# State-space stage of a hybrid decoder step: B and C convolved before x, fixed convolution tiles, column copies on ScalarE, sums of squares emitted later

## The chip, the cores and the metric

One core of one Trainium2 chip runs one inference step of one decoder layer. The metric is the device time of one execution in microseconds (us), the median of three runs. PE is TensorE, ACT is ScalarE, DVE is VectorE, POOL is GpSimd, SP is the queue that issues most DMAs.

## The reference, cut to what matters

Each of 544 token rows (512 of a prompt, 8 sequences of 4 of a sample) goes through a feed-forward block, a mixing block of a state-space branch and an attention branch, a cross-attention over a memory, and a second feed-forward block, each with norms before and after. The change lies in the state-space branch and in the norms of the mixing and memory blocks:

```python
def causal_dwconv(xbc, buf, w, b):
    l = xbc.shape[1]
    xp = jnp.concatenate([buf.astype(xbc.dtype), xbc], axis=1)
    y = b
    for j in range(SSD_CONV_W):            # 4 taps
        y = y + w[j] * xp[:, j:j + l]
    return jax.nn.silu(y), xp[:, l:]
```

The convolution runs over 4096 channels: 2048 of x, 1024 of B and 1024 of C. Behind it, 32 heads in 8 groups are scanned in chunks of 128 tokens: `cb = C B^T` in a chunk, times a decay, times x; plus the state that is carried from chunk to chunk, which B and x make and C reads. The result is gated with silu(z) and normalised over the 256 channels of a group.

## The kernel before, in words

Activations stand with channels on the 128 partitions and the 544 tokens along the row. Matrix products are made from split operands (a rounded high part and the remainder, three products for each), so one product of 128 output channels over 1024 inputs is 48 matmuls of 256 or 288 columns (`mm`, L310). Weights come by `weights` (L251): two DMAs on SP into `wr`, a cast on ACT to `wh` (L270), a subtraction on DVE or POOL to `wl` (L271).

The program is written as generators that `weave` (L104) interleaves by a clock of estimated costs: `yield cost, delay` says how much PE work was emitted and how long its generator is to be left alone. The framework then makes from it one fixed list of instructions for each engine, in which it may move ready work ahead. Each engine works through its list in order.

The state-space stage is `ssd` (L1241). For each of the 8 groups (0 to 7 here) `fronts` runs `ssd_x` (L1291) and `ssd_z` (L1278), `tails` runs `ssd_y` (L1334), and beside them run the lists and the attention of the sample (`sample_select`, `sample_att`), whose rows are fetched by DMAs that POOL issues (L1613).

- `ssd_x` makes four products for a group, in the order x, x, B, C. The result in PSUM is copied by ACT into a tile `CB` of 604 columns (L1312); POOL writes three zeros ahead of the prompt (L1311), the old columns of the sample (L1315) and the new columns of the sample (L1316), and keeps the last columns for an output (L1317, L1318). The convolution is one ACT instruction (L1322) and three on DVE (L1324); then a tanh on ACT (L1326) and a last product on DVE (L1327) make `XO`. POOL copies the sample's columns of `XO` into `XS`, three times over for x and B (L1329).
- `ssd_y` starts with `pcb` (L1347, products of C and B by chunk) and `pbt` (L1353, B turned), then `pxt` (L1362, the two tiles of x turned) and `pcs` (L1379 and L1380, the sample's columns turned, and B times C of the sample). It ends with the norm of a group: `st` (L341, sums of squares), a chain of small DVE instructions in `rsqrt`, `zt` (L352) and `psr` (L355).

`bound` (L372) is the step between two blocks for one half of the tokens: it takes the norm behind the block (`sth` on `sqf`, L419, then `pgr`, L439), adds it to `hT`, sums the squares of the new `hT` on ACT and POOL (L369, L370, tile `sqh`), and takes the next norm (`sth` on `sqh`). `project` (L1762) calls it with a tile `rt` for w_out and for w_mo, once for each half.

Of the kernel before, what the change touches and what calls it, by code (L numbers as in the profile page):

```python
# [7 lines left out]
F32 = mybir.dt.float32  # L8
# [18 lines left out]
C_Z, C_X, C_B, C_C, C_DT, C_Q, C_K, C_V, C_QI, C_KI, C_WI, C_GS, C_GA = (  # L27
    0, 2048, 4096, 5120, 6144, 6176, 7200, 7456, 7712, 8224, 8288, 8296, 9320)
# [140 lines left out]
class Net:  # L169
# [202 lines left out]
    def bound(self, half, sq, post_g, pre_g, rt=None):  # L372


        nc, hT, y = self.nc, self.hT, self.y
        r0, n = HALF[half]
        sl = slice(r0, r0 + n)
        if post_g is not None:
            yield 0.0, 3.0
            r = yield from self.rms_h(sq, half)  # L380
        if pre_g is not None:
            acc = self.nw.tile([P, 288], F32, tag="sqh", name="sqh", bufs=2)
        for k in range(8):
            if post_g is not None:
                nc.vector.scalar_tensor_tensor(y[:, k, sl], y[:, k, sl], post_g[:, k:k + 1], r, op0=ALU.mult, op1=ALU.mult)
                (nc.gpsimd if k % 2 else nc.vector).tensor_tensor(hT[:, k, sl], hT[:, k, sl], y[:, k, sl], op=ALU.add)
            if pre_g is not None:
                self.sq_acc(acc, hT[:, k, sl], n, k == 0, last=(k == 7))
            if rt is not None:
                g = pre_g[:, k:k + 1]  # L390
                nc.scalar.activation(self.uh[:, k, sl], hT[:, k, sl], AF.Copy, scale=g)
                nc.vector.scalar_tensor_tensor(self.ul[:, k, sl], hT[:, k, sl], g, self.uh[:, k, sl].bitcast(F32), op0=ALU.mult, op1=ALU.subtract)
            yield 0.0, 1.0
        if pre_g is None:
            return
        yield 0.0, 4.0
        r = yield from self.rms_h(acc, half)
        if rt is not None:
            nc.scalar.copy(rt[:, sl], r)
            return  # L400
        for k in range(8):
            u = self.nw.tile([P, 288], F32, tag="u", name="u", bufs=2)
            nc.vector.scalar_tensor_tensor(u[:, :n], hT[:, k, sl], pre_g[:, k:k + 1], r, op0=ALU.mult, op1=ALU.mult)
            self.split(self.uh[:, k, sl], self.ul[:, k, sl], u[:, :n], nc.gpsimd if k % 4 == 3 else None)
            yield 0.0, 0.9
# [835 lines left out]
    def ssd(self, sel_ex, rounds):  # L1241
        nc, I = self.nc, self.I
        ex, fx = ExitStack(), ExitStack()
        self.sp = self.pool("ssd", ex)
        self.fp = self.pool("ssdf", fx)
        self.fr, self.zt = {}, {}
        self.r32 = self.sp.tile([P, 32], F32, name="r32")
        for q in range(4):
            nc.vector.tensor_copy(self.r32[q * 32:(q + 1) * 32], self.ident[q * 32:(q + 1) * 32, q * 32:(q + 1) * 32])
        fs = Flag()  # L1250
        f_x, f_y, f_z = ([Flag() for _ in range(8)] for _ in range(3))

        def tails():
            for g in range(8):
                yield from f_x[g].wait()
                yield from f_y[g].after(self.ssd_y(g, f_z[g]))

        def fronts():
            for g in range(8):
                if g >= 2:  # L1260
                    yield from f_y[g - 2].wait()
                yield from f_x[g].after(self.ssd_x(g))
                yield from f_z[g].after(self.ssd_z(g))
                if g in (1, 2):
# [26 lines left out]
    def ssd_x(self, g):  # L1291

        nc, I, sp = self.nc, self.I, self.sp
        fp = self.fp
        w_in = I["w_in"][0]
        wx = self.win(C_X + g * 256)
        h0 = []
        for i in range(2):
            h = sp.tile([P, 8, P], F32, tag="h0", name="h0", bufs=2)
            nc.sync.dma_start(h, I["state_ssm"][0][:, 4 * g + 2 * i:4 * g + 2 * i + 2].rearrange("b h p n -> (h p) b n"))  # L1300
            h0.append(h)
        XO = []
        xt = sp.tile([P, 320], F32, tag="XS", name="XS", bufs=2)
        XS = [xt[:, q * 96:q * 96 + (96 if q < 3 else 32)] for q in range(4)]
        for q in range(4):
            ct = (2 * g, 2 * g + 1, 16 + g, 24 + g)[q]
            if q == 2:
                wb = self.weights(("bc", g), [w_in[:, C_B + g * P:C_B + (g + 1) * P], w_in[:, C_C + g * P:C_C + (g + 1) * P]], 8)
            ps = yield from self.mm(wx if q < 2 else wb, self.xs, (q % 2) * P)
            CB = fp.tile([P, 604], F32, tag="CB", name="CB", bufs=2)  # L1310
            nc.gpsimd.memset(CB[:, 0:3], 0.0)  # L1311
            nc.scalar.copy(CB[:, 3:547], ps)  # L1312
            sb = CB[:, 547:603].rearrange("p (b j) -> p b j", b=8)
            raw = CB[:, 515:547].rearrange("p (b j) -> p b j", b=8)
            nc.gpsimd.tensor_copy(sb[:, :, 0:3], self.sc[:, ct, :].rearrange("p (b j) -> p b j", b=8))  # L1315
            nc.gpsimd.tensor_copy(sb[:, :, 3:7], raw)  # L1316
            nc.gpsimd.tensor_copy(self.ncv[:, ct, 0:3], CB[:, 512:515])  # L1317
            nc.gpsimd.tensor_copy(self.ncv[:, ct, 3:27].rearrange("p (b j) -> p b j", b=8), raw[:, :, 1:4])  # L1318
            pool = sp if g % 2 else fp
            xo = pool.tile([P, 600], F32, tag=f"XO{q}", name=f"XO{q}")  # L1320
            cw = lambda j: self.convw[:, j * 32 + ct:j * 32 + ct + 1]
            nc.scalar.activation(xo, CB[:, 0:600], AF.Identity, scale=cw(0), bias=self.convb[:, ct:ct + 1])  # L1322
            for j in range(1, 4):
# [2 lines left out]
            nc.scalar.activation(th, xo, AF.Tanh)  # L1326
            nc.vector.scalar_tensor_tensor(xo, th, 1.0, xo, op0=ALU.add, op1=ALU.mult)  # L1327
            r = 3 if q < 3 else 1
            nc.gpsimd.tensor_copy(XS[q].rearrange("p (r b t) -> p r b t", r=r, b=8),  # L1329
                                  xo[:, 544:600].rearrange("p (b j) -> p b j", b=8)[:, :, 3:7].unsqueeze(1).broadcast_to([P, r, 8, 4]))  # L1330
            XO.append(xo)
        self.fr[g] = (XO, XS, h0)

    def ssd_y(self, g, z):  # L1334
        nc, I, O, sp = self.nc, self.I, self.O, self.sp
        XO, XS, h0 = self.fr[g]
# [8 lines left out]
        ps = self.ps1("pcb")  # L1345
# [5 lines left out]
        ps = self.ps1("pbt")  # L1351
        for c in range(4):
            nc.tensor.transpose(ps[:, c * P:(c + 1) * P], BO[:, c * P:(c + 1) * P], self.ident)  # L1353
        Bt = sp.tile([P, 4, P], F32, tag="hT_", name="Bt", bufs=2)
        nc.scalar.copy(Bt.rearrange("p a b -> p (a b)"), ps)
        hcol = lambda t: t.rearrange("p (c h) -> p c h", c=4)[:, :, 4 * g:4 * g + 4]
        xd = sp.tile([P, 4, 4, 64], F32, tag="xd", name="xd")
        xe = sp.tile([P, 4, 4, 64], F32, tag="xe", name="xe")
        for i in range(2):
            ps = self.ps1("pxt")  # L1360
# [36 lines left out]
        Bb = sp.tile([96, 8, P], F32R, tag="Bb", name="Bb")  # L1397
        for b in range(8):
            nc.scalar.activation(Bb[:, b, :], Bs.bitcast(F32), AF.Copy, scale=self.bmask[:, b:b + 1])
        yield 0.5, 5.0  # L1400
        CZ = sp.tile([P, 288], F32, tag="CZ", name="CZ")
        nc.gpsimd.memset(CZ, 0.0)
        nc.gpsimd.tensor_copy(CZ.rearrange("p (b x) -> p b x", x=36)[:, :, :4], XS[3].rearrange("p (b t) -> p b t", b=8))
# [676 lines left out]
```

## Time and profile before

| | |
|---|---|
| median of 3 runs | 2214.59 us (2214.11 to 2221.61) |
| the profiled execution | 2221.14 us, span 2219.4 us |
| PE busy | 2112.4 us, 95% of the span |
| DVE, ACT, POOL busy | 1319.2, 947.8, 457.9 us |
| state-space stage | about 830 to 1400 us of the span |
| mean granted TensorE clock | 0.974 |

PE is busy nearly all the time, so a change is worth what it takes from or adds to PE's idle time, and from the time in which PE runs at the lower of its two clocks. The granted clock is given as a share of 2.4 GHz: 0.50 is 1.2 GHz.

### The profile page before, as it was taken

To read this page: it belongs to the slowest core of one execution; us is meant where nothing else is said; L and a number is where in the kernel's file an instruction comes from. 1 tells how busy PE (TensorE), PEld (TensorE's weight loads), DVE (VectorE), ACT (ScalarE), POOL (GpSimd) and SP (SyncE) were. 2 spreads that over 40 slices of the span, in tenths; PEclk is the share of its full clock that TensorE was granted. 3 is DMA by queue.
4 is the path that set the end of the run, shared out by engine and by line. 5 is a ranking of instruction groups with operands and counts; after the bars stand their busy time and mean duration, and the time that the engine had idled before them with its cause. 6 is when DMAs were issued, how large, how long until landed. Compare 5 with 4: busy or idle time off the path is not lost.

```text
span 2219.4 us, 41174 instructions
## 1 busy us (share of the span) xinstructions
PE 2112.4 (95%) x16675; PEld 1967.7 (89%) x16675; DVE 1319.2 (59%) x2711; ACT 947.8 (43%) x1757; POOL 457.9 (21%) x555
## 2 busy tenths in 40 slices
PE   7999999999999999999999999999999979999998
PEld 7999999998887779888778788999987879999998
DVE  6543334574788889886675678554663475423445
ACT  6323345345336665444345355332535343222233
POOL 0000011132123202235564451012320320000011
PEclk9999999999999999999899899999999989999999
DMA  6424565447432233345455545564444433233243
GB/s 194 128 82 127 172 209 187 120 124 223 141 118 78 83 93 100 116 146 177 125 158 163 152 143 166 174 201 148 139 161 142 150 116 115 71 92 95 82 123 106
DMA packets 320106, 301.70 MB, mean 136 GB/s; under 512 B 25416, under 2 KB 290632, under 8 KB 318868
## 3 DMA queue, kind: packets, MB, share of 16 engines
q1 hardware_dynamic: 310508, 272.58, 40.3%
q0 software_dynamic: 8448, 25.18, 3.7%
q8 instruction: 131, 2.15, 0.4%
q10 hardware_dynamic: 960, 1.31, 0.2%
q14 instruction: 59, 0.48, 0.1%
HBM read 261.14 MB, written 37.35 MB: 134 GB/s over the span
## 4 chain that ended last, share of the span: by engine, by line
PE 67%; DVE 13%; DMA 6%; ACT 6%; POOL 4%; issue 4%; SPq 0%; DVEq 0%; POOLq 0%; ACTq 0%
PE pg L310 38%; PE pgh L310 14%; PE pmo L591 2%; DVE wl L271 2%; ACT wh L270 2%; DVE XO L1324 1%; POOL kv L1613 1%; DVE gtm L1077 1%; DMA abc<-ac_d 1%; DMA yt<-yssd_d 1%; POOL sqh L370 1%; PE pmkT L1806 1%; DMA wr<-in_ffn_wu 1%; ACT abc L1372 1%; DVE eqm L1120 1%
## 5 line engine op out<-in xcount | busy, mean ns | idle before, releaser
L270 ACT CAST wh<-wr 128x1024 fp32r<-128x1024 f32 (+3 forms) x362 | 341.4, 958 | 513.4 <-PE pg L310 297.9
L271 DVE TENSOR_TENSOR wl<-wr,wh 128x1024 fp32r<-128x1024 f32 (+3 forms) x338 | 388.6, 1163 | 220.9 <-ACT wh L270 213.1
L310 PE MATMUL pg<-uh,wh 128*128 128x256 f32 (+1 forms) x2336 | 503.1, 296 | 2.0 <-DVE zt L1287 2.0
L310 PE MATMUL pg<-uh,wl 128*128 128x256 f32 (+1 forms) x2336 | 494.8, 292 | 0.0
L310 PE MATMUL pg<-ul,wh 128*128 128x256 f32 (+1 forms) x2336 | 494.1, 292 | 0.0
L310 PEld LDWEIGHTS pg<-uh,wh 128*128 128x128 f32 x2336 | 381.5, 191 | 21.0 <-issue 16.0
L310 PEld LDWEIGHTS pg<-ul,wh 128*128 128x128 f32 x2336 | 382.1, 191 | 3.3 <-issue 2.2
L310 PEld LDWEIGHTS pg<-uh,wl 128*128 128x128 f32 x2336 | 380.7, 190 | 2.9 <-issue 2.4
L310 PE MATMUL pgh<-uh,wh 128*128 128x288 f32 (+2 forms) x880 | 261.5, 300 | 11.2 <-ACT wh L270 7.5
L310 PE MATMUL pgh<-uh,wl 128*128 128x256 f32 (+2 forms) x880 | 259.9, 297 | 6.8 <-DVE wl L271 6.8
L310 PE MATMUL pgh<-ul,wh 128*128 128x256 f32 (+1 forms) x880 | 257.4, 294 | 0.0
L310 PEld LDWEIGHTS pgh<-uh,wh 128*128 128x128 f32 (+1 forms) x880 | 171.0, 195 | 14.9 <-ACT wh L270 8.5
L310 PEld LDWEIGHTS pgh<-uh,wl 128*128 128x128 f32 (+1 forms) x880 | 169.8, 193 | 10.6 <-DVE wl L271 9.1
L310 PEld LDWEIGHTS pgh<-ul,wh 128*128 128x128 f32 x880 | 171.7, 195 | 1.1 <-issue 0.8
L370 POOL TENSOR_TENSOR sqf<-sqf,sqt 128x256 f32<-128x256 f32 (+1 forms) x48 | 52.4, 1092 | 514.1 <-ACT sqt L369 513.8
L310 PE MATMUL pgh<-hh,wh 128*128 128x288 f32 (+1 forms) x352 | 101.7, 289 | 0.0
L310 PE MATMUL pgh<-hh,wl 128*128 128x288 f32 (+1 forms) x352 | 101.0, 287 | 0.2 <-DVE wl L271 0.2
L310 PE MATMUL pgh<-hl,wh 128*128 128x288 f32 (+1 forms) x352 | 100.9, 287 | 0.0
L1324 DVE SCALAR_TENSOR_TENSOR XO<-CB,convw,XO 128x600 f32<-128x600 f32 x96 | 84.9, 885 | 23.4 <-ACT XO L1322 22.8
L702 POOL DMA_INDIRECT G<-in_cache_kidx,ix x16 | 17.0, 1060 | 361.0 <-DVE ix L697 281.5
L620 DVE TENSOR_TENSOR g<-pg,g 128x544 f32<-128x544 f32 x32 | 23.2, 726 | 98.9 <-PE pg L310 98.9
L617 DVE TENSOR_TENSOR g<-pg,rt 128x544 f32<-128x544 f32 x32 | 23.2, 725 | 98.7 <-PE pg L310 98.7
(608 smaller groups left out, 3885.5 us busy)
## 6 DMA issues: line engine op xcount, KB each, us to landing
wr<-in_w_in SPq DMA_DIRECT2D x66, 512.0 KB
wr<-in_ffn_wg SPq DMA_DIRECT2D x48, 512.0 KB
wr<-in_ffn_wu SPq DMA_DIRECT2D x48, 512.0 KB
wr<-in_ffn_wd SPq DMA_DIRECT2D x44, 384.0 KB
wr<-in_ffn_wd SPq DMA_DIRECT2D x44, 320.0 KB
kt_d<-KT SPq DMA_DIRECT2D x8, 1024.0 KB
KT<-kt_d SPq DMA_DIRECT2D x16, 512.0 KB
wr<-in_w_in SPq DMA_DIRECT2D x32, 256.0 KB
```

The costliest lines, as they stand in the source:

```text
L270: nc.scalar.copy(hi[:, s], r)
L271: (lo_eng or nc.vector).tensor_tensor(lo[:, s], r, hi[:, s].bitcast(F32), op=ALU.subtract)
L310: nc.tensor.matmul(o, a[:, k, c0:c0 + m], x[:, r0:r0 + n], start=(k == 0 and j == 0), stop=(k == KT - 1 and j == 2))
L370: (nc.vector if last else nc.gpsimd).tensor_tensor(acc[:, :n], acc[:, :n], s[:, :n], op=ALU.add)
L591: nc.tensor.matmul(ps[:, :256], a[:, k, i * P:(i + 1) * P], b[:, k, :], start=(k == 0 and j == 0), stop=(k == 7 and j == 2))
L617: nc.vector.tensor_tensor(g1[:, :n], pg, rt[:, sl], op=ALU.mult)
L620: nc.vector.tensor_tensor(g1[:, :n], pu, g1[:, :n], op=ALU.mult)
L1077: nc.vector.scalar_tensor_tensor(G, S, thr[:, j:j + 1], one, op0=ALU.is_ge, op1=ALU.mult, accum_out=cnt[:, j:j + 1])
L1120: nc.vector.max_index(self.IX[:, r * 8:(r + 1) * 8], at[:, r * 8:(r + 1) * 8], S)
L1324: nc.vector.scalar_tensor_tensor(xo, CB[:, j:j + 600], cw(j), xo, op0=ALU.mult, op1=ALU.add)
L1372: nc.scalar.activation(abc[i][:, h, c * P:(c + 1) * P], abc[i][:, h, c * P:(c + 1) * P], AF.Relu, scale=-1.0, bias=self.acs[:, col:col + 1])
L1613: nc.gpsimd.indirect_dma_start(out=t[:, hf, :], out_offset=None, in_=(pk, pv)[x], in_offset=off)
```

## The change

- Two tiles `CB` are allocated once for the stage, with their three zeros written once; before, each of the 32 convolutions took a tile from a rotation of two and wrote the zeros again.
- In `ssd_x` the order of the four products is B, C, x, x. The weights of B and C are asked for at the start, those of x behind C.
- The new columns of the sample are copied by ACT from PSUM (before: by POOL from `CB`), and the old ones by POOL ahead of the product. `XS` is copied by ACT.
- `ssd_y` yields once more behind `pbt`, and for 2.5 in place of 5.0 behind `Bb`.
- In `bound`, where `rt` is given, the delay ahead of the sums of squares is 8.0 in place of 4.0.

```diff
-        yield 0.0, 4.0
+        yield 0.0, 4.0 if rt is None else 8.0
         r = yield from self.rms_h(acc, half)
...
+        self.CB = [self.fp.tile([P, 604], F32, name=f"CB{i}") for i in range(2)]
+        for t in self.CB:
+            nc.gpsimd.memset(t[:, 0:3], 0.0)
...
-        wx = self.win(C_X + g * 256)
+        wb = self.weights(("bc", g), [w_in[:, C_B + g * P:C_B + (g + 1) * P], w_in[:, C_C + g * P:C_C + (g + 1) * P]], 8)
...
-        for q in range(4):
+        XO = [None] * 4
+
+        for q in (2, 3, 0, 1):
             ct = (2 * g, 2 * g + 1, 16 + g, 24 + g)[q]
-            if q == 2:
-                wb = self.weights(("bc", g), [w_in[:, C_B + g * P:C_B + (g + 1) * P], w_in[:, C_C + g * P:C_C + (g + 1) * P]], 8)
+            CB = self.CB[q % 2]
+            sb = CB[:, 547:603].rearrange("p (b j) -> p b j", b=8)
+            nc.gpsimd.tensor_copy(sb[:, :, 0:3], self.sc[:, ct, :].rearrange("p (b j) -> p b j", b=8))
             ps = yield from self.mm(wx if q < 2 else wb, self.xs, (q % 2) * P)
-            CB = fp.tile([P, 604], F32, tag="CB", name="CB", bufs=2)
-            nc.gpsimd.memset(CB[:, 0:3], 0.0)
             nc.scalar.copy(CB[:, 3:547], ps)
-            sb = CB[:, 547:603].rearrange("p (b j) -> p b j", b=8)
+            nc.scalar.copy(sb[:, :, 3:7], ps[:, TP:].rearrange("p (b j) -> p b j", b=8))
             raw = CB[:, 515:547].rearrange("p (b j) -> p b j", b=8)
-            nc.gpsimd.tensor_copy(sb[:, :, 0:3], self.sc[:, ct, :].rearrange("p (b j) -> p b j", b=8))
-            nc.gpsimd.tensor_copy(sb[:, :, 3:7], raw)
...
-            nc.gpsimd.tensor_copy(XS[q].rearrange("p (r b t) -> p r b t", r=r, b=8),
-                                  xo[:, 544:600].rearrange("p (b j) -> p b j", b=8)[:, :, 3:7].unsqueeze(1).broadcast_to([P, r, 8, 4]))
-            XO.append(xo)
+            nc.scalar.copy(XS[q].rearrange("p (r b t) -> p r b t", r=r, b=8),
+                           xo[:, 544:600].rearrange("p (b j) -> p b j", b=8)[:, :, 3:7].unsqueeze(1).broadcast_to([P, r, 8, 4]))
+            XO[q] = xo
+            if q == 3:
+                wx = self.win(C_X + g * 256)
...
         nc.scalar.copy(Bt.rearrange("p a b -> p (a b)"), ps)
+        yield 0.5, 2.5
...
-        yield 0.5, 5.0
+        yield 0.5, 2.5
         CZ = sp.tile([P, 288], F32, tag="CZ", name="CZ")
```

The lists of the engines change with it at many places. Three of them are shown.

DVE, the start of group 2, before. `XO_10742` is C of the group; `cb` is the first DVE instruction that needs `pcb`, and `dum`, `row` and `mk` belong to `sample_select`.

```order
L1324 SCALAR_TENSOR_TENSOR XO_10742<-CB,convw,XO_10742 128x600
L1562 TENSOR_TENSOR row<-row,dum 128x256
L1565 SCALAR_TENSOR_TENSOR mk<-pgf,own 128x256
L1561 TENSOR_SCALAR dum<-pgf,ptf 128x256
L1327 SCALAR_TENSOR_TENSOR XO_10742<-th,XO_10742 128x600
L1562 TENSOR_TENSOR row<-row,dum 128x256
L1287 SCALAR_TENSOR_TENSOR zt_10904<-zt_10904,pg 128x544
L1561 TENSOR_SCALAR dum<-pgf,ptf 128x256
L1349 TENSOR_TENSOR cb<-pcb,tri 128x512
```

The same place after the change, where `XO_10722` is the second tile of x and L1329 its last product:

```order
L1353 TENSOR_TENSOR cb<-pcb,tri 128x512
L1566 TENSOR_SCALAR dum<-pgf,ptf 128x256
L1326 SCALAR_TENSOR_TENSOR XO_10722<-CB_8948,convw,XO_10722 128x600
L1567 TENSOR_TENSOR row<-row,dum 128x256
L1326 SCALAR_TENSOR_TENSOR XO_10722<-CB_8948,convw,XO_10722 128x600
L1566 TENSOR_SCALAR dum<-pgf,ptf 128x256
L1326 SCALAR_TENSOR_TENSOR XO_10722<-CB_8948,convw,XO_10722 128x600
L1567 TENSOR_TENSOR row<-row,dum 128x256
L1368 TENSOR_TENSOR xd<-pxt,dt 128x4x128
L1329 SCALAR_TENSOR_TENSOR XO_10722<-th,XO_10722 128x600
```

What moved: `cb` and the first `xd` now stand ahead of the last convolution of the group; they stood behind it.

ACT, the start of group 0, before. `th` is the tanh, `zt_9390` and `zt_9483` are the two tiles of z, `wh` the casts of weights, `Bb` eight scaled copies of B of the sample.

```order
L1326 ACTIVATE th<-XO_9172 128x600
L1286 ACTIVATE zt_9390<-pg 128x544
L1326 ACTIVATE th<-XO_9238 128x600
L1355 COPY Bt<-pbt 128x512
L270 CAST wh<-wr 128x1024
L1286 ACTIVATE zt_9483<-pg 128x544
L270 CAST wh<-wr 128x1024
L1411 COPY H<-pst 128x256
L1399 ACTIVATE Bb<-Bs,bmask 96x128 x8
```

The same place after the change:

```order
L1359 COPY Bt<-pbt 128x512
L270 CAST wh<-wr 128x1024
L1331 COPY XS<-XO_9170 128x96
L1328 ACTIVATE th<-XO_9234 128x600
L1290 ACTIVATE zt_9386<-pg 128x544
L1331 COPY XS<-XO_9234 128x96
L1416 COPY H<-pst 128x256
L1404 ACTIVATE Bb<-Bs,bmask 96x128 x8
L1440 COPY hT__9458<-ph_9453 128x512
L1440 COPY hT__9465<-ph_9460 128x512
L270 CAST wh<-wr 128x1024
L1290 ACTIVATE zt_9479<-pg 128x544
```

What moved: copies of `XS` stand between the other work, and the casts for the next group's first product stand behind `Bb`, where they stood ahead of it.

PE, the end of the w_out product of the second half, before. `pmkT` are turned blocks of the memory's keys, `sth` the sums of squares of the first half.

```order
L1806 MATMUL pmkT<-ident,mb 128x128 x8
L419 MATMUL sth<-ones,sqh 128x1 x2
L1806 MATMUL pmkT<-ident,mb 128x128 x4
```

And after the change:

```order
L1811 MATMUL pmkT<-ident,mb 128x128 x20
L310 MATMUL pgh<-uh,wh 128x256
L310 MATMUL pgh<-ul,wh 128x256
L1811 MATMUL pmkT<-ident,mb 128x128 x4
L419 MATMUL sth<-ones,sqh 128x1 x2
```

What moved: `sth` stands behind 24 turned blocks and two matmuls, where it stood behind 8 blocks. The sums of squares of the second half stand there behind 109 matmuls and 4 blocks, counted from the `pgr` ahead of them (before: 107 and 8). In the memory block's own norm, `sth` of the first half stands where it stood.

## Rows read from the trace of the kernel before

**Rows 1.** The page, busy time by engine.

```profile
PE 2112.4 (95%) x16675; PEld 1967.7 (89%) x16675; DVE 1319.2 (59%) x2711; ACT 947.8 (43%) x1757; POOL 457.9 (21%) x555
```

**Rows 2.** PE's waits, 860 to 1400 us: who for whom, total us, times, longest.

```profile
PE psr L355 <- DVE zt L352: 9.8, 5, 3.2
PE pcb L1347 <- DVE XO L1327: 9.8, 3, 4.7
PE pO L1683 <- DMA kv<-in_cache_v,slot: 5.3, 4, 2.6
PE pcs L1380 <- POOL XS L1329: 3.8, 1, 3.8
```

**Rows 3.** Timeline of PE, starts of groups 0, 2, 3, 4: start, us, line, [idle before].

```profile
861.34 2.08 PE L1347 MATMUL pcb<-XO,XO 128*128 128x128 f32 x8 [2.59 <-DVE XO L1327]
...
992.73 1.65 PE L1347 MATMUL pcb<-XO,XO 128*128 128x128 f32 x6 [4.74 <-DVE XO L1327]
...
1085.09 1.22 PE L1347 MATMUL pcb<-XO,XO 128*128 128x128 f32 x4 [2.47 <-DVE XO L1327]
...
1158.54 0.31 PE L1380 MATMUL pcs<-XS 128*32 128x32 f32 x2 [3.75 <-POOL XS L1329]
```

**Rows 4.** Windows: us, busy (count) PE, PEld, DVE, ACT, POOL; PEclk; DMA; GB/s.

```profile
992.00:994.00 2.00, 1.27 (x6) 1.27 (x7) 1.91 (x4) 0.35 (x1) 0.55 (x2) 0.50 0.27 82
994.00:996.00 2.00, 2.00 (x11) 2.00 (x11) 1.02 (x2) 0.30 (x1) 0.38 (x1) 0.50 0.00 0
996.00:998.00 2.00, 2.00 (x13) 1.71 (x11) 1.45 (x3) 0.29 (x1) 2.00 (x1) 0.60 0.00 0
1158.00:1160.00 2.00, 1.46 (x7) 1.40 (x8) 1.11 (x3) 0.00 (x0) 1.94 (x6) 0.51 0.21 66
1160.00:1162.00 2.00, 2.00 (x22) 1.48 (x20) 1.97 (x5) 0.00 (x0) 1.08 (x1) 0.50 0.00 0
1162.00:1164.00 2.00, 2.00 (x10) 1.51 (x5) 0.87 (x3) 0.59 (x3) 1.19 (x2) 0.50 0.00 0
900.00:910.00 10.00, 10.00 (x83) 9.97 (x82) 8.43 (x18) 10.00 (x22) 2.44 (x10) 1.00 0.29 99
```

**Rows 5.** Tile CB: its POOL copies, ns min/median/max.

```profile
L1316 POOL COPY CB<-CB x32: 207/225/2942, 831.3 to 1354.3; 128x32 f32<-128x32 f32 x32
```

**Rows 6.** Timeline of ACT, convolutions of groups 3 and 5 that waited for POOL.

```profile
1079.96 0.89 ACT L1322 ACTIVATE XO<-CB,gains,convw 128x600 f32<-128x600 f32 x1 [4.87 <-POOL CB L1316]
...
1211.01 0.89 ACT L1322 ACTIVATE XO<-CB,gains,convw 128x600 f32<-128x600 f32 x1 [2.37 <-POOL CB L1316]
```

**Rows 7.** Timeline of POOL and DVE in group 2, ahead of its `pcb`.

```profile
981.83 2.49 POOL L271 TENSOR_TENSOR wl<-wr,wh 128x1024 fp32r<-128x1024 f32 x1
...
986.98 2.42 POOL L271 TENSOR_TENSOR wl<-wr,wh 128x1024 fp32r<-128x1024 f32 x1 [1.48 <-ACT wh L270]
...
982.58 2.38 DVE L1327 SCALAR_TENSOR_TENSOR XO<-th,XO 128x600 f32<-128x600 f32 x1 [0.52 <-ACT th L1326]
985.99 0.84 DVE L1324 SCALAR_TENSOR_TENSOR XO<-CB,convw,XO 128x600 f32<-128x600 f32 x1 [1.03 <-ACT XO L1322]
...
987.09 2.94 DVE L1324 SCALAR_TENSOR_TENSOR XO<-CB,convw,XO 128x600 f32<-128x600 f32 x1
...
994.85 0.69 DVE L1349 TENSOR_TENSOR cb<-pcb,tri 128x512 f32<-128x512 f32 x1 [0.94 <-PE pcb L1347]
```

**Rows 8.** Timeline of PE: the norm of group 4, in the front of group 5.

```profile
1219.51 1.22 PE L355 MATMUL psr<-zt,ones 128*128 128x512 f32 x1 [2.10 <-DVE zt L352]
```

**Rows 9.** Timeline of PE: sums of squares behind w_out, first and second half.

```profile
1593.35 0.58 PE L419 MATMUL sth<-ones,sqh 128*128 128x1 f32 x4 [2.81 <-DVE sqh L370]
...
1628.55 0.77 PE L419 MATMUL sth<-ones,sqh 128*128 128x1 f32 x6 [3.98 <-DVE sqh L370]
1629.25 1.12 PE L1806 MATMUL pmkT<-ident,mb 128*128 128x128 f32 x4
```

**Rows 10.** Groups of ACT: busy us, mean ns, idle before (the two below the first: 860 to 1400 us).

```profile
L875 ACT ACTIVATE hb<-hb 128x32 f32<-128x32 f32 x1 | 0.2, 229 | 0.0
...
L270 ACT CAST wh<-wr 128x1024 fp32r<-128x1024 f32 x50 | 51.9, 1047 | 30.7 <-PE pg L310 30.1 <-issue 0.6
L1399 ACT ACTIVATE Bb<-Bs,bmask 96x128 fp32r<-96x128 f32 x64 | 19.6, 391 | 11.3 <-DVE Bs L1396 11.3
```

More of the change, by code (lines that the diff above doesn't have):

```diff
@@ L1301, in ssd_x @@
             h0.append(h)
-        XO = []
         xt = sp.tile([P, 320], F32, tag="XS", name="XS", bufs=2)
         XS = [xt[:, q * 96:q * 96 + (96 if q < 3 else 32)] for q in range(4)]
-        for q in range(4):
+        XO = [None] * 4
+        for q in (2, 3, 0, 1):
             ct = (2 * g, 2 * g + 1, 16 + g, 24 + g)[q]
-            if q == 2:
-                wb = self.weights(("bc", g), [w_in[:, C_B + g * P:C_B + (g + 1) * P], w_in[:, C_C + g * P:C_C + (g + 1) * P]], 8)
+            CB = self.CB[q % 2]
+            sb = CB[:, 547:603].rearrange("p (b j) -> p b j", b=8)
+            nc.gpsimd.tensor_copy(sb[:, :, 0:3], self.sc[:, ct, :].rearrange("p (b j) -> p b j", b=8))
             ps = yield from self.mm(wx if q < 2 else wb, self.xs, (q % 2) * P)
-            CB = fp.tile([P, 604], F32, tag="CB", name="CB", bufs=2)
-            nc.gpsimd.memset(CB[:, 0:3], 0.0)
             nc.scalar.copy(CB[:, 3:547], ps)
-            sb = CB[:, 547:603].rearrange("p (b j) -> p b j", b=8)
+            nc.scalar.copy(sb[:, :, 3:7], ps[:, TP:].rearrange("p (b j) -> p b j", b=8))
             raw = CB[:, 515:547].rearrange("p (b j) -> p b j", b=8)
-            nc.gpsimd.tensor_copy(sb[:, :, 0:3], self.sc[:, ct, :].rearrange("p (b j) -> p b j", b=8))
-            nc.gpsimd.tensor_copy(sb[:, :, 3:7], raw)
             nc.gpsimd.tensor_copy(self.ncv[:, ct, 0:3], CB[:, 512:515])
```

## The prediction

> **What bounds the kernel.** I begin with the page's busy times. PE is busy for 95% of the span and no other engine for more than 59% [rows 1]. So an edit on ACT, DVE or POOL is worth what it takes from PE's idle time, and no more. The second view is the list of PE's waits in the stage that changes, 860 to 1400 us, which names them: `psr` waits for DVE 9.8 us, `pcb` for DVE 9.8, `pO` for DMAs 5.3, and `pcs` for POOL 3.8 [rows 2]. The third is the timeline, for when they occur: `pcb` waits at the starts of groups 0, 2 and 3, `pcs` in group 4 [rows 3]. The fourth is the windows: behind a wait PE runs on at the lower clock for some microseconds. From 992 to 996 us the granted clock is 0.50, from 996 to 998 it is 0.60, and from 1158 to 1164 about 0.50, where PE at work has 1.00 [rows 4]. PE works at half pace there, so a wait costs more than its own length.
>
> **The profiled execution and the median.** The sum is made against the profiled execution, 2221.14 us, which is 6.5 us above the median, 2214.59. I subtract the same gain from the median. 0.5%, about what a measurement of this kernel can tell from no change, is 11.1 us.
>
> **A. Group starts.** The three `pcb` waits are 2.59 + 4.74 + 2.47 = 9.80 us, the `pcs` wait is 3.75: 13.55 together [rows 3]. The clock behind them: in group 2 PE worked 1.27 us of the first window and 2.00 of the second at half pace, and 2.00 at 0.60, so it lost 1.27 x 0.5 + 1.0 + 2.0 x 0.4 = 2.4 us. In group 4 it lost 1.46 x 0.49 + 1.0 + 1.0 = 2.7 [rows 4]. For the two shorter waits I estimate 1.5 each. The whole prize is 13.55 + 8.1 = 21.7 us.
>
> `pcb` needs B and C. In the new order C comes two products earlier. 83 matmuls take 10.00 us [rows 4], so one takes 0.12, a product of 48 takes 5.8, and 11.6 us of PE work lie between: more than any of these waits, so `pcb` no longer waits. What is late next is the second `pxt`, which needs the second tile of x. I go through the groups.
>
> - *Group 4.* `pcs` waited for POOL's copies of `XS`. They are on ACT now, which in that stretch has little to do (0.00, 0.00 and 0.59 us busy in the three windows [rows 4]). I take the whole: 3.75 + 2.7 = 6.5 gained.
> - *Group 3.* ACT's convolution waited 4.87 us for POOL's copy into `CB` [rows 6]. One such copy has taken 2942 ns where the median is 225 [rows 5], and its place is in POOL's queue behind longer work. It becomes an ACT copy of about 0.23 (the nearest row is 128x32 on ACT at 229 ns [rows 10]). The chain gets some 4.6 us shorter. Against that DVE now does `cb`, at 0.69 [rows 7], and some of `xd`, `xe` and the products behind them, at 0.69 or less each, ahead of the last convolution: I take 3.3. That leaves over 1 us, and `pxt` stands about 2 us further on in PE's list than `pcb` did. The wait of 2.47 goes: with its clock 4.0 gained.
> - *Group 2.* Here the chain is on DVE. Two instructions took 2.38 and 2.94 us where the same shape takes 0.84 beside them, 3.6 us too long, and beside each a subtraction ran on POOL, from 981.83 for 2.49 us and from 986.98 for 2.42 [rows 7]. The change leaves POOL's subtractions. It removes DVE's idle 1.03 behind ACT [rows 7], and PE comes later: 54 full and 12 small matmuls lie between product and consumer in place of 59, about 2.4 us more. It adds `cb` and one `xd`, 1.4 us. The residual is 4.74 + 1.4 - 1.0 - 2.4 = 2.7 us, still long enough for the clock to fall: 2.0 gained.
> - *Group 0.* DVE is the chain again. What stands ahead of its last product shrinks by about 1.1 us, and PE's place hardly changes: residual about 1.5; 1.1 and half of the clock's 1.5 gained, 1.8.
> - *Groups 4 to 7* have no `pcb` wait to lose but get the later `pxt`: I charge 0.5 each, 2.0. The bounds are 0 and 1.5 each.
>
> A: 6.5 + 4.0 + 2.0 + 1.8 - 2.0 = **12.3 us** gained, of 21.7.
>
> *The rule on the shared port.* The Trainium skill, "SBUF — State Buffer", section "Who interferes with whom", says that a DVE instruction with two inputs in SBUF and a GpSimd instruction that reads SBUF exclude each other, the loser waiting for the whole instruction. By it the stretched pair in group 2 stays for as long as POOL subtracts there, and moving POOL's copies of 207 to 225 ns would free little. The trace agrees here: both stretched instructions read two tiles and end within 0.7 us of POOL's subtraction, and the one of 0.84 has no subtraction beside it [rows 7].
>
> **B. Norms of a group.** `psr` waited 2.10 us in group 4 [rows 8], where ACT's convolution in the next front stood 2.37 us for POOL [rows 6] and DVE's instructions behind it stand ahead of the norm's chain. That goes, with an estimated 1.5 of clock: 3.6. In the new order `psr` of group 3 has 36 matmuls of the products ahead of it (54 before), less the 10 of `pO` that come in, and that of group 5 also moves closer: I charge 1.5 and 1.0. The remaining `psr` waits, 9.8 - 2.1 = 7.7 us [rows 2], stay. B: **1.1 gained**; bounds 5 lost and 6 gained.
>
> **C. Sums of squares.** Behind w_out the first half waited 2.81 us, the second 3.98; four turned blocks take 1.12 [rows 9], so 0.28 each. The first gets 16 blocks and two matmuls more ahead, 4.7 us: its 2.81 goes, with an estimated 1.0 of clock. The second loses four blocks (1.1) and gains two matmuls (0.2): 0.9 longer. In the memory block the place of `sth` is the same: nothing. C: 2.81 + 1.0 - 0.9 = **2.9 gained**; bounds 1 and 4.
>
> **D. ACT's added copies.** 32 column copies and 32 `XS` copies at 0.23 are 14.7 us more on ACT, which is busy 947.8 of 2219 [rows 1]: cover enough on average. One place is not average. In group 0 the casts of the next product's weights (`wh`, 1.05 us each) now stand behind eight `Bb` of 0.39, 3.1 us, which wait for DVE's `Bs` [rows 10]. I charge 1.5 for a new wait of PE there; bounds 0 and 6. The fixed tiles save 30 short memsets on POOL, nothing on PE's path. The shorter yields only move instructions, which the order has counted.
>
> **Sum.** 12.3 + 1.1 + 2.9 - 1.5 = 14.8 us. 2221.1 - 14.8 = 2206.3 for an execution like the profiled one; 2214.6 - 14.8 = 2199.8 for the median. **Forecast 2200 us.**
>
> **Rivals.**
>
> *The waits only change their name* (0.26). DVE is nearly full where groups begin (8.43 of 10.00 us [rows 4]), and C first changes only which tile it is late with. Then groups 0 and 2 gain nothing and `pxt` waits 1.5 in groups 4 to 7: A is 6.5 + 4.0 - 6.0 = 4.5, the sum 4.5 + 1.1 + 2.9 - 1.5 = 7.0, the time 2207.6. This is also the case in which the change doesn't do what it says: a convolution still waits for one of two `CB`. For it: rows 7, where DVE's own instructions make the delay. Against it: groups 3 and 4, where POOL's copies are shown as the cause.
>
> *Everything goes* (0.15). If the stretched pair in group 2 was chance, or shifts, and `pxt` comes late enough everywhere, A is 21.7; B 3.6, as no norm comes nearer in effect; C 2.9; D nothing: 28.2, 2186.4. For it: the 11.6 us that C moves ahead. Against it: the last x tile has no more PE work behind it than C had.
>
> *ACT's queue becomes the bound, slower* (0.08). The `XS` copies on ACT wait for DVE's last product, in order, and the casts of the next weights queue behind them. No such wait is among the longest of this stage [rows 2], so each would be new. If PE waits for `wh` 2.0 us in all eight groups, and 1.5 of clock each, that is 28 us against the 16.3 gained without D: 11.7 slower, 2226.3. It decides once these waits pass 16.3 / 8 = 2.0 us a group with their clock. For it: in group 0 the order does put casts behind `Bb`. Against it: ACT is 43% busy and a copy takes 0.23.
>
> **How the numbers follow.** The forecast's case has 0.51; its own range, from the bounds of groups 4 to 7, B and D, is 2193 to 2206. About eight tenths of it lie below 2203.5 (0.5% faster): 0.41. With 0.15 of everything gone and a little (0.04) of the changed names, faster is 0.60. The rest of the forecast, 0.10, most of the changed names, 0.22, and 0.02 of ACT's case are within 0.5%: 0.34. Slower by over 0.5% is the rest of ACT's case: 0.06. The range of 8 in 10 leaves out that case and the tails of two others: 2184 to 2217.
>
> **What would show it.** Right: `pcb` without a wait at all eight starts; the second `pxt` with up to 3 us in groups 0 and 2, none in group 3; `pcs` without a wait for POOL; the first `sth` behind w_out without a wait and the second with 4 to 5 us; POOL's busy time down, ACT's up by about 15 us; `psr` waits of 6 to 10 us in all. Wrong: waits of PE for `wh` (ACT's case), `pxt` waits of over 10 us in all (changed names), or a granted clock below 0.974 on average though the waits went. A POOL subtraction that lands on DVE's chain in another group would also make it wrong, since no row tells where these fall after the change.

## The result and the profile after

| | before | after |
|---|---|---|
| median of 6 runs, us | 2215.12 | 2200.77 (2197.83 to 2205.22) |
| ratio, 95% interval | | 0.9935, 0.992 to 0.9949 |
| span of the profiled execution, us | 2219.4 | 2199.4 |
| mean granted clock | 0.974 | 0.979 |

The change is 14.4 us faster; 14.8 had been forecast. The total was right. Its parts were not all right, as the experiments show. The profiled pair lies 20.0 us apart, more than the medians, so times of single places are read for where they lie, and the ratio for how much.

The page's busy times after the change, which answer to [rows 1]:

```profile
PE 2101.4 (96%) x16675; PEld 1960.6 (89%) x16675; DVE 1324.2 (60%) x2711; ACT 955.2 (43%) x1821; POOL 444.4 (20%) x461
```

POOL lost 13.5 us and 94 instructions, ACT gained 7.4 us and 64. PE does the same 16675 matmuls in 11 us less of busy time: that is the clock, granted at 0.974 before and 0.979 after.

The stage and what follows it, from 830 us up to the norm of w_out's result (its first `sth` is at 1567.2 us before, at 1549.6 after), before and then after (views of windows; columns as in [rows 4]):

```profile
830.00:1567.00 737.00, 696.93 (x5678) 638.19 (x5677) 500.80 (x1006) 316.87 (x581) 260.82 (x371) 0.96 0.50 152
```

```profile
830.00:1549.00 719.00, 687.89 (x5688) 633.33 (x5688) 507.26 (x1010) 324.90 (x647) 250.34 (x281) 0.97 0.52 156
```

The same work is done in 18 us less. PE's idle time, stretch less busy, falls from 40.1 to 31.1 us: 9.0. Its busy time falls by another 9.0, because the clock is at its lower level for less long (windows of 2 us, each one's busy time times the missing share of the clock, summed, give 23.8 us before and 15.4 after). So in this pair half of the gain is the clock behind the waits; the prediction had priced it at 8.1 of 21.7 us in part A. A second chip agrees: in the runs with the delay alone and with the delay undone (below) the stretch from 831 us to that `sth` takes 746 and 732 us, with 7.8 us less idle time and 6.2 less busy time.

PE's waits in the stage after the change, which answer to [rows 2]:

```profile
PE pxt L1367 <- DVE XO L1329: 10.4, 3, 5.3
PE psr L355 <- DVE zt L352: 7.0, 3, 3.7
PE pO L1681 <- DVE PN L1677: 3.7, 1, 3.7
...
PE pO L1688 <- DMA kv<-in_cache_v,slot: 0.8, 2, 0.4
```

`pcb` is gone from the list, and so is `pcs`. `pxt` has come with 10.4 us, `psr` went from 9.8 to 7.0, the waits of `pO` for DMAs from 5.3 to 0.8 and for `PN` from two of 1.0 to one of 3.7. The `pxt` waits on the timeline of PE, groups 0, 2 and 5, answer to [rows 3]:

```profile
862.08 0.66 PE L1367 MATMUL pxt<-ident,XO 128*128 128x128 f32 x4 [1.06 <-DVE XO L1329]
...
994.67 1.11 PE L1367 MATMUL pxt<-ident,XO 128*128 128x128 f32 x4 [5.34 <-DVE XO L1329]
...
1218.75 0.65 PE L1367 MATMUL pxt<-ident,XO 128*128 128x128 f32 x4 [4.03 <-DVE XO L1329]
```

Group 2 waits longer than before (5.34 against 4.74), and group 5 has a wait that is new. Why shows in rows of DVE there, and of POOL's work beside them, first in group 2 and then in group 5:

```profile
982.75 2.37 DVE L1329 SCALAR_TENSOR_TENSOR XO<-th,XO 128x600 f32<-128x600 f32 x1 [0.51 <-ACT th L1328]
...
987.94 2.95 DVE L1326 SCALAR_TENSOR_TENSOR XO<-CB,convw,XO 128x600 f32<-128x600 f32 x1
...
982.00 2.47 POOL L271 TENSOR_TENSOR wl<-wr,wh 128x1024 fp32r<-128x1024 f32 x1
...
987.83 2.42 POOL L1380 TENSOR_TENSOR abc<-abc,cb 128x1024 f32<-128x1024 f32 x1
...
1213.43 5.26 DVE L1329 SCALAR_TENSOR_TENSOR XO<-th,XO 128x600 f32<-128x600 f32 x1
...
1213.38 4.66 POOL L1380 TENSOR_TENSOR abc<-abc,cb 128x1024 f32<-128x1024 f32 x2
```

In group 5 an instruction of 0.78 us takes 5.26, for as long as POOL multiplies the two `abc`. In group 2 a subtraction and an `abc` hold two more, 1.6 and 2.1 us too long. In the old order `cb`, and with it `abc`, came behind the last convolution of its group. Now `cb` is early, and POOL's `abc` runs beside the convolutions of x. I counted, on DVE's timeline from 820 to 1420 us, the instructions that took over 0.5 us longer than the same instruction does where POOL has neither `abc` nor subtractions beside it (its median in the run with both edits, below; two overlapping copies `qz` of 64x16, 0.8 and 0.9 us, are left out). Before there are 10, 18.0 us too long together: 6 are `Gs` (the sample's decay times its `cb`), to which no wait of PE is put down, 3 are instructions on `XO`, 5.9 us. After there are 13, 25.0 us, and 6 of them are on `XO`, 13.0 us. Nine of the 13 lie beside `abc`, four beside POOL's subtractions. The change takes waits away, and moves the hold onto the instructions that the next wait is for.

Behind w_out (timeline of PE, answers to [rows 9]) the first `sth` has no wait, and two others stand in its place:

```profile
1575.52 0.66 PE L1811 MATMUL pmkT<-ident,mb 128*128 128x128 f32 x4 [2.14 <-ACT y L1779]
1577.77 0.66 PE L1811 MATMUL pmkT<-ident,mb 128*128 128x128 f32 x4 [1.59 <-ACT mkT__16911 L1812]
...
1615.33 0.80 PE L419 MATMUL sth<-ones,sqh 128*128 128x1 f32 x6 [3.81 <-DVE sqh L370]
```

The turned blocks that were put ahead of `sth` wait for ACT, 3.73 us together, against the 2.81 that went.

### The profile page after: what moved, and what is told of

Read it like the earlier page. It is cut to its first block, busy times and chain, and to the rows that moved or that the text cites. A ratio compares the mean times of both kernels' runs of the same rounds, so it can differ in the third digit from the quotient of the medians.

```text
span 2199.4 us, 41232 instructions
## 1 busy us (share of the span) xinstructions
PE 2101.4 (96%) x16675; PEld 1960.6 (89%) x16675; DVE 1324.2 (60%) x2711; ACT 955.2 (43%) x1821; POOL 444.4 (20%) x461
## 4 chain that ended last, share of the span: by engine, by line
PE 72%; DVE 13%; DMA 6%; ACT 4%; issue 3%; POOL 2%; SPq 0%; DVEq 0%; ACTq 0%; POOLq 0%
PE pg L310 42%; PE pgh L310 14%; PE pmo L591 2%; DVE wl L271 2%; ACT wh L270 2%; DMA wr<-in_ffn_wu 1%; DVE gtm L1077 1%; DVE XO L1326 1%; DMA yt<-yssd_d 1%; DMA abc<-ac_d 1%; PE pmkT L1811 1%; POOL sqh L370 1%; PE pmo L1878 1%; DVE XO L1329 1%; DMA wr<-in_ffn_wg 1%
```

## Experiments

They ran on several chips, on which the kernel before took 2217 to 2235 us; only ratios to runs of before on the same chip are compared, and 0.5% is 11 us. Three parts of the change are taken apart first: the delay, the order with its tiles and yields, and the copies on ACT.

**The delay alone.** Edit on the kernel before:

```diff
-        yield 0.0, 4.0
+        yield 0.0, 4.0 if rt is None else 8.0
```

> The kernel before with one edit: the sums of squares behind w_out and w_mo are emitted after a delay of 8.0 in place of 4.0. By the prediction's term C it is 2.9 us faster than before (ratio 0.9987): the wait of the first sth behind w_out, 2.81 us, goes, and the second grows from 3.98 to about 4.9. Rival (from the profile of the changed kernel, where the first sth has no wait, but pmkT waits 2.14 and 1.59 us for ACT ahead of it and the second sth still waits 3.81): nothing is gained, the idle time only moves to the turned blocks; 0 to 2 us slower up to the end of w_out, ratio 0.999 to 1.001.

Measured: 1.001, 0.9993 to 1.0027. No gain. The first `sth` has no wait, `pmkT` waits 2.14 and 1.14 us, the second `sth` 3.77. The rival holds.

**The delay undone in the changed kernel.**

```diff
-        yield 0.0, 4.0 if rt is None else 8.0
+        yield 0.0, 4.0
```

> The changed kernel with the delay back at 4.0; the order of the state-space stage is the changed kernel's to the instruction. By the prediction (A, B and D carry 11.9 of 14.8 us) it is 2.9 us slower than the changed kernel, about 2203.5, ratio to before 0.995. Rival: the state-space stage carries the whole gain and more (17 us in the profiled pair), the delay gives nothing: ratio to before 0.992 to 0.994, with the first sth waiting about 2.8 us again and pmkT not waiting.

Measured: 0.9915, 0.9888 to 0.9942. The first `sth` waits 2.83 us again, and `pmkT` only 0.38. The stage carries the whole gain, and the delay nothing that can be measured.

**The order alone.** On the changed kernel, with the delay at 4.0:

```diff
-            nc.scalar.copy(sb[:, :, 3:7], ps[:, TP:].rearrange("p (b j) -> p b j", b=8))
             raw = CB[:, 515:547].rearrange("p (b j) -> p b j", b=8)
+            nc.gpsimd.tensor_copy(sb[:, :, 3:7], raw)
...
-            nc.scalar.copy(XS[q].rearrange("p (r b t) -> p r b t", r=r, b=8),
+            nc.gpsimd.tensor_copy(XS[q].rearrange("p (r b t) -> p r b t", r=r, b=8),
```

> The changed order (B, C, x, x, fixed tiles, the changed yields), but both column copies stay on POOL and the delay is 4.0. By the prediction's terms the order alone takes the pcb waits (9.8 us and their clock) and gives pxt waits: groups 0 and 2 gain 3.8, groups 4 to 7 lose 2.0, group 3 keeps part of its wait behind POOL, the norms that come nearer lose 2.5: about 2 us faster, ratio 0.998 to 1.0. Rival: the order itself carries the gain, since C's 11.6 us of distance is what takes the waits, and the copies matter little: 10 us or more faster, ratio 0.9955 or less.

Measured: 1.0021, 1.0006 to 1.0036: a little slower than before. PE's waits in the stage of this run:

```profile
PE pxt L1367 <- DVE XO L1329: 14.8, 4, 6.8
PE pcs L1384 <- POOL XS L1331: 13.4, 4, 5.0
PE psr L355 <- DVE zt L352: 5.8, 3, 3.8
```

Neither side had it: both expected a gain. The `pcb` waits are gone, and `pcs` and `pxt` wait 28 us in their place. x is now convolved last, and its copy into `XS` is the last thing ahead of `pcs`; on POOL it stands behind other work.

**The copies alone.** On the kernel before:

```diff
             nc.scalar.copy(CB[:, 3:547], ps)
+            nc.scalar.copy(CB[:, 547:603].rearrange("p (b j) -> p b j", b=8)[:, :, 3:7], ps[:, TP:].rearrange("p (b j) -> p b j", b=8))
...
-            nc.gpsimd.tensor_copy(sb[:, :, 3:7], raw)
...
-            nc.gpsimd.tensor_copy(XS[q].rearrange("p (r b t) -> p r b t", r=r, b=8),
+            nc.scalar.copy(XS[q].rearrange("p (r b t) -> p r b t", r=r, b=8),
```

> The kernel before with both column copies on ACT and nothing else: old order x, x, B, C, rotating tiles, delay 4.0. By the prediction's terms POOL's copies cost 6.5 us in group 4 (pcs), about 4.0 in group 3 (pcb behind ACT's convolution that waited 4.87) and 3.6 in the norm of group 4: 14 less at most 1.5 on ACT's queue, about 12.6 us faster, ratio 0.9943; pcb still waits in groups 0 and 2 (2.6 and 4.7 us). Rival: without the new order the copies save only the pcs wait, DVE stays late with C: 5 us or less, ratio 0.998 or more.

Measured: 0.9986, 0.9968 to 1.0005. Neither side's mechanism is right, though the rival's figure holds. `pcs` no longer waits for POOL and `pcb` waits 4.6 us in place of 9.8, as the theory had it. At the `psr` of group 4 this run is 6.4 us ahead of the run with the delay alone, whose stage is the kernel's before and which ran on the same chip (1217.28 against 1223.74 us). At the first `sth` only 2.7 of them are left. In between lie these waits of its timeline, for gathers of `sample_att` and for ACT:

```profile
1242.95 0.42 PE L1683 MATMUL pO<-kv,PZ 128*32 128x128 f32 x8 [3.51 <-DMA kv<-in_cache_v,slot]
...
1245.89 0.65 PE L1683 MATMUL pO<-kv,PZ 128*32 128x128 f32 x6 [1.45 <-DMA kv<-in_cache_v,slot]
...
1253.77 0.43 PE L1442 MATMUL pys<-hT__13680,CZ 128*32 128x128 f32 x8 [2.53 <-ACT hT__13680 L1435]
```

The gathers do not take the lead away: at the last `pO` shown it is still 7.1 us (1245.89 against 1253.00 us). The wait for `hT` behind it is one that the other run does not have; at the next `pO` 4.1 us are left (1258.66 against 1262.74).

So neither part alone is worth anything that can be measured, and both together are 0.65 to 0.85%. Which of the two copies does it, was asked in the changed kernel.

**One copy back on POOL: the new columns.** The first two lines of the edit of the order alone, in the changed kernel.

> The changed kernel with one of its two column copies back on POOL: the new columns of the sample in CB, ahead of the convolution; XS stays on ACT. Theory (what the new order needs is XS on ACT, since x's XS is now the last thing ahead of pcs; with both copies on POOL pcs waited 13.4 us in four places): most of the gain stays, ratio to before 0.993 to 0.996, no pcs wait for XS. Rival (the prediction's reading of group 3, in which a convolution stood 4.87 us behind POOL's copy into CB): the convolution waits for POOL again, pxt and psr get later, and half of the gain or more is lost, ratio 0.997 or more.

Measured: 0.9986, 0.9974 to 0.9998. My theory fell, the rival holds. `pcs` has no wait, but `pxt` waits 17.9 us in four places, since ACT's convolution waits for POOL's copy again, 14.3 us in 14 waits, where the changed kernel has none; as here in group 2 (timeline of ACT):

```profile
982.67 0.89 ACT L1324 ACTIVATE XO<-CB,gains,convw 128x600 f32<-128x600 f32 x1 [2.51 <-POOL CB L1318]
```

**One copy back on POOL: `XS`.** The last two lines of that edit.

> The changed kernel with the other copy back on POOL: XS; the new columns in CB stay on ACT. Theory: pcs waits for POOL's XS copies of x behind abc and the gathers, over 8 us in several places, and the gain is gone: ratio to before 0.998 to 1.002. Rival: it is the copy into CB that matters, and the ratio stays at 0.993 to 0.996.

Measured: 1.0044, 1.003 to 1.0058, slower than before. The theory's mechanism holds, at a higher price than it gave. `pcs` waits 13.7 us in three places, the longest 6.35 in group 3. POOL's timeline there, after the last product of x had started on DVE at 1086.00 us for 0.77:

```profile
1087.90 0.95 POOL L1618 DMA_INDIRECT kv<-in_cache_k,slot  x1 [0.30 <-issue]
...
1090.12 2.37 POOL L1380 TENSOR_TENSOR abc<-abc,cb 128x1024 f32<-128x1024 f32 x1
1092.65 0.98 POOL L1618 DMA_INDIRECT kv<-in_cache_k,slot  x1 [0.16 <-issue]
...
1097.54 0.26 POOL L1331 COPY XS<-XO 128x96 f32<-128x96 f32 x1
```

The copy of 0.26 us starts 10.8 us after its data is there, behind gathers of about 1.3 us each and an `abc`. With `abc` and the subtractions on POOL, both copies are needed on ACT for this order.

**POOL's hold on DVE.** The last group of runs goes back to the 13 DVE instructions. It has the changed kernel itself as its base.

> The changed kernel itself, as the base for the three runs beside it: ratio to before 0.992 to 0.995, with pxt waiting about 10 us for XO in three places, the longest in group 2 (5.3) and group 5 (4.0).

Measured: 0.9933, 0.9908 to 0.9958, and `pxt` waits of 1.57, 5.34 and 4.04 us. Other waits differ between chips and executions: with the same instructions PE is idle for 39.9 us here (830 to 1557 us), where it was 31.1 in the profile of the result, so times of what follows are compared within this chip. In the stage no wait of PE, ACT or DVE is put down to POOL, here or in that profile, and 1.4 us of PE's here (3.0 there) go to gathers that POOL issues: a shorter queue of POOL has little to give to the next edits.

The products on DVE:

```diff
-            (nc.vector if 1 <= g <= 4 and i else nc.gpsimd).tensor_tensor(abc[i], abc[i], cb.rearrange("p c t -> p (c t)").unsqueeze(1).broadcast_to([P, 2, TP]), op=ALU.mult)
+            nc.vector.tensor_tensor(abc[i], abc[i], cb.rearrange("p c t -> p (c t)").unsqueeze(1).broadcast_to([P, 2, TP]), op=ALU.mult)
```

> The changed kernel with all 16 products of abc and cb on DVE (before: 12 on POOL at 2.39 us, 4 on DVE at 1.22). Theory (POOL's products hold up DVE's two-input instructions that run beside them): the last product of XO in group 5, 5.26 us beside two abc of 4.66 together on POOL, falls to 0.8; its pxt wait of 4.03 goes with some 2 us of clock behind it: 4 to 6 us faster than the changed kernel. Rival (DVE is simply too full where groups begin): 12 more instructions of 1.22 on DVE, 14.6 us, make pxt and psr later; pxt waits 10 us or more in all, and the time is the same or up to 5 us longer.

Measured: 0.9871, 0.9846 to 0.9897; on this chip 2204.9 against 2215.7 us for the changed kernel. The convolutions on DVE (view of the tile `XO`: ns, minimum, median and maximum), in the changed kernel (the profile of the result) and then in this run:

```profile
L1326 DVE SCALAR_TENSOR_TENSOR XO<-CB,convw,XO x96: 820/839/2971, 835.2 to 1344.2; 128x600 f32<-128x600 f32 x96
L1329 DVE SCALAR_TENSOR_TENSOR XO<-th,XO x32: 752/784/5261, 841.4 to 1346.2; 128x600 f32<-128x600 f32 x32
```

```profile
L1326 DVE SCALAR_TENSOR_TENSOR XO<-CB,convw,XO x96: 818/836/880, 833.2 to 1345.3; 128x600 f32<-128x600 f32 x96
L1329 DVE SCALAR_TENSOR_TENSOR XO<-th,XO x32: 760/782/785, 839.2 to 1347.4; 128x600 f32<-128x600 f32 x32
```

The medians are the same, the maxima have gone, and `pxt` has no long wait left. 12 products that took 2.39 us on POOL take 1.22 on DVE. The gain, 10.8 us, is twice what the theory gave: the pxt waits of all three groups went, not that of group 5 alone. The two profiled executions show it in the stage: at the first `sth` this one is 7.6 us ahead (1550.10 against 1557.73 us), though the two end only 0.9 us apart. Four DVE instructions are still held, all beside subtractions, but none of them on `XO`. New are waits of `pst` for ACT's `H`, 6.5 us in three places.

The gates' subtractions in groups 1 and 2 on DVE:

```diff
-            w = self.win((C_GS, C_GA)[x] + c * 256, lo_eng=self.nc.gpsimd)
+            w = self.win((C_GS, C_GA)[x] + c * 256, lo_eng=None if x and c >= 2 else self.nc.gpsimd)
```

> The changed kernel with the weight subtractions of the two gates that fall into groups 1 and 2 on DVE in place of POOL (8 subtractions, 2.4 us each on POOL, 1.22 on DVE). Theory of POOL's hold on DVE: in group 2 the product of 2.37 us and the instruction of 2.04 us fall to their usual 0.8 and 0.35, the pxt wait of 5.34 to about 2.5: 2.5 to 4 us faster than the changed kernel. Rival (DVE too full): the subtractions on DVE take what the holds took, the wait stays at 4 to 6.

Measured: 0.9901, 0.9877 to 0.9925; 2211.4 us, 4.3 less than the changed kernel, though the intervals of the two overlap. In group 2 the `pxt` wait of 5.34 is gone, and two of 1.68 and 3.57 us for `zt` and one of 2.50 for `row` have come. (It was 4 subtractions that moved, not 8.) Eight DVE instructions are still held, all beside `abc`, besides two `qz`; among them the `dum` that the theory wanted back at 0.35 us, which takes 1.88. Group 5 keeps its 4.05: its cause is `abc`.

Both edits:

> Both edits. Theory: no DVE instruction on XO over 1 us in groups 2 and 5, pxt waits under 3 us in all, 7 to 10 us faster than the changed kernel, so about 0.3 to 0.45% of the time. Rival (DVE too full): 24 us more of DVE work in the stage, waits for DVE as long as in the changed kernel or longer, the same time or slower.

Measured: 0.9843, 0.9817 to 0.9869; 2200.7 us, 15.0 less than the changed kernel beside it. This kernel is faster than the kernel before and than the changed one. But for two copies `qz` of 0.8 and 0.9 us, not one DVE instruction of the stage is over 0.5 us longer than its median. `pst` waits 5.4 us for ACT's `H` here too. The page's busy times, of the changed kernel beside it and of this run:

```profile
PE 2103.8 (95%) x16675; PEld 1962.6 (89%) x16675; DVE 1321.9 (60%) x2711; ACT 956.9 (43%) x1821; POOL 444.1 (20%) x461
```

```profile
PE 2101.3 (96%) x16675; PEld 1960.0 (89%) x16675; DVE 1316.3 (60%) x2727; ACT 956.9 (44%) x1821; POOL 400.3 (18%) x445
```

DVE has 16 instructions more and is busy no longer: the added work is paid by the time that it was held.

Both edits on the kernel before, without the change:

> The kernel before, with the products of abc and the two gates' subtractions on DVE, nothing of the change. Theory (in the old order these POOL instructions meet few convolutions: four DVE instructions were held up by 7.9 us together, against 13 by 25 us in the changed kernel): it gains the held-up pair of group 2 and little else, 2 to 6 us, ratio to before 0.997 to 0.999, and the changed order is needed for the rest. Rival (POOL's hold on DVE is the whole matter, whatever the order): pcb and psr waits mostly go, as in the changed kernel with both edits: ratio 0.990 or less.

Measured: 1.0025, 1.0012 to 1.0038, slower. No DVE instruction is held up, and `pcb` waits 1.7 us in place of 9.8. More had been held up in the old order than the theory counted, 10 by 18.0 us and not 4 by 7.9: the median of `Gs` that it was counted by is itself a held one, as the view of the tile `Gs` shows (ns, minimum, median and maximum; the kernel before, then this run):

```profile
L1386 DVE TENSOR_TENSOR Gs<-dec_s,cbs x8: 268/1900/2294, 867.7 to 1370.0; 32x128 f32<-32x128 f32 x8
```

```profile
L1386 DVE TENSOR_TENSOR Gs<-dec_s,cbs x8: 268/270/271, 866.2 to 1371.7; 32x128 f32<-32x128 f32 x8
```

All of it went, and nothing was gained. `pO` now waits 12.5 us for gathers (5.3 before), `pslot` 3.9 for DVE, and `pcs` still 3.9 for POOL's `XS`. Both sides had the sign wrong. The gathers are not later than in the profile before, which is of another chip. The batch of the longest wait (first row, PE) starts on POOL at 1308.80 us, before at 1313.03 (second and third row):

```profile
1317.97 0.43 PE L1683 MATMUL pO<-kv,PZ 128*32 128x128 f32 x8 [3.97 <-DMA kv<-in_cache_v,slot]
...
1308.80 1.23 POOL L1613 DMA_INDIRECT kv<-in_cache_v,slot  x1 [10.99 <-PE pO L1683]
...
1313.03 1.02 POOL L1613 DMA_INDIRECT kv<-in_cache_v,slot  x1 [3.63 <-PE pO L1683]
```

PE comes to it earlier still: in its list 8 matmuls of products stand between this batch's 16 `pO` and the 16 ahead of them, where 24 stood before.

Both edits on the order alone (copies on POOL, delay 4.0):

> The changed order with both column copies on POOL (as in the run of the order alone, ratio 1.0021), and with abc and the two gates' subtractions on DVE. It tells what on POOL the copies stand behind. Theory (gathers: eight in a row of about 1.3 us each stand ahead of an XS copy, as in group 3 of the run with XS on POOL): pcs still waits for XS, 6 us or more in all, DVE's held-up instructions are gone, ratio 0.995 to 1.000; ACT's copies are needed in any case. Rival (the long products and subtractions are what blocks POOL's queue): with them gone the copies are on time, pcs waits under 3 us in all, and the ratio comes down to 0.984 to 0.990, as with both edits on the changed kernel.

Measured: 0.9921, 0.9903 to 0.9939. The mechanism of the theory holds, its size does not: `pcs` still waits 10.0 us in three long waits, of 2.98, 3.84 and 3.19 (the profile puts the 3.84 down to POOL's `XS`, the others to nothing that it shows), and 1.3 in two short ones, yet the kernel is as fast as the changed one. Against the order alone, 1.0021, the two edits are worth 1.0%; ACT's copies on top of them another 0.8%.

The ratios side by side, the new order with either delay, since that measured nothing:

| order | copies on | abc, gates on | ratio |
|---|---|---|---|
| old | POOL | POOL | 1 |
| old | ACT | POOL | 0.9986 |
| old | POOL | DVE | 1.0025 |
| new | POOL | POOL | 1.0021 |
| new | ACT | POOL | 0.9915 to 0.9935 |
| new | POOL | DVE | 0.9921 |
| new | ACT | DVE | 0.9843 |

In the old order neither of the two, taken off POOL by itself, pays. In the new one each does. The old order with both was not run, so how much of the last line needs the new order is not shown.

## Why the prediction was right, and where it was not

**What bounds the kernel** held: PE's idle time and the clock behind the waits give the gain of the stage, 17.6 of the 20.0 us of the profiled pair.

**A, group starts.** Forecast 12.3 us. In the profiled pair the waits fell from 13.55 us (`pcb` and `pcs`) to 10.43 (`pxt`), and the busy time lost to the clock right behind them from 9.4 to 3.3 (here and under B: windows of 0.25 us, busy time times the missing share of the clock): 9.2 us. `pcb` without a wait at all eight starts, `pcs` without one, group 3 without one: right. The residual of group 2 was put at 2.7 and measured at 5.34; group 0's at 1.5 and measured at 1.06; groups 4 to 7 were charged 0.5 each, and measured 4.03 in group 5 and no wait of 0.5 in the others. The step that failed there is the sentence that DVE's added work costs `cb` and one `xd`, 1.4 us. It left out that an early `cb` lets POOL's `abc` run beside the convolutions, which is 5.26 us for one instruction. The Trainium skill, "SBUF — State Buffer", section "Who interferes with whom", says that a DVE instruction with two inputs in SBUF contends with a GpSimd instruction that reads SBUF; I had applied it to POOL's subtractions alone. The trace agrees with it in both: of the 13 held instructions 4 are left with `abc` on DVE, 8 are left with the subtractions there, and none with both. Twelve of the 13 read two tiles; the other, `dum`, reads one and a column of scalars.

How the gain splits over the change's parts also failed. I gave 6.5 us in group 4 and most of 4.0 in group 3 to the copies, which, with 3.6 from B and less 1.5 for ACT, made them worth 12.6 us by themselves, and the order 2. Measured by themselves they are worth 3 us (-1 to 7) and -5 us. The two are not a sum: the new order is worth something only when x's columns don't stand in POOL's queue behind long work, which either the copies on ACT or the products and subtractions on DVE bring about, and the copies only when what they free is not met by the next wait, of which the old order has several (`pcb` for DVE, `hT` for ACT).

**B, norms.** Forecast 1.1 gained, `psr` 6 to 10 us in all: 7.0, right as a sum of waits. As a price it was far off: the waits fell by 2.8 us and the clock behind them cost 12.1 us before and 4.5 after, 10.4 together. Most of that belongs to this execution: in the run with the delay alone, whose stage is the kernel's before, the clock behind `psr` cost 4.8 us. Group 4's wait fell from 2.10 to 0.51 and not to nothing, and those of groups 3 and 5, charged 2.5, did not come.

**C, sums of squares.** Forecast 2.9 gained, measured nothing: 1.001 alone. The failing step is that the turned blocks put ahead of `sth` cost nothing. They wait for ACT, which empties PSUM for them (`y` and `mkT`), 2.14 and 1.59 us. The blocks were also priced too high: 0.28 us each was read from 1629.25 us on, where the granted clock was 0.77 and then 0.50; twelve of them took 1.47 us ahead of `sth` after the change, at 1.00. The term's bounds, 1 to 4, did not hold zero.

**D, ACT.** The 1.5 charged in group 0 did not come: no wait for `wh` in the stage. ACT's busy time rose by 7.4 us, not by 15: the 64 copies take 14.6 us by their own rows, as charged, but they overlap with their neighbours on ACT.

So A gave less than forecast, C nothing, B more in the profiled pair, and D's charge did not come. The errors have opposite signs, and that the total was met to half a microsecond is luck. What it also holds, and no term had, are the waits of `pO`: for gathers 4.5 us less, for `PN` 1.8 more.

**The rivals.** ACT's queue as the bound: refuted, no wait for `wh`. Waits that only change their name: the sign set for it, `pxt` waits of over 10 us in all, came (10.4), though not its time; right in groups 2 and 5, and it is what the order alone does (1.0021). Everything goes: not reached by the change, but the version with both edits is 1.57% faster than before, more than that rival's 28 us.

## What to carry to other kernels

A reordering that makes a tile ready earlier also lets its consumers on other engines start earlier; look at what they run beside, POOL's two-input work beside DVE's above all. Short copies that stand between two engines' steps belong on an engine whose queue is short: a copy of 0.26 us on POOL came 10.8 us late. Parts of a change that remove successive waits on one path are not worth their sum: measure them together and apart.

## What the runs showed of the hardware

Twelve products of 128x1024 take 2.39 us each on POOL and 1.22 on DVE, and while two ran on POOL a DVE instruction of 0.78 us took 5.26. With them and four subtractions of 128x1024 moved to DVE, DVE's busy time went from 1321.9 to 1316.3 us, where they alone are 16 times 1.22, 19.5 us. POOL is held as well: after the change four of its `abc` took 2.9 to 3.3 us, beside instructions on `XO` or a DVE subtraction; before, none took over 2.46.
